# Attention logits as three rounded-float products of high and low parts, with heads 4 to 7 turned late into the slots of heads 0 to 3

## The chip, the cores and the metric

The kernel runs on one core of a Trainium2 chip. The metric is the time of one execution on the device in microseconds (us). Six engines matter: TensorE (PE in the profile; its weight loads are listed apart as PEld), VectorE (DVE), ScalarE (ACT), GpSimd (POOL) and SyncE (SP), which only issues transfers. Each engine works through its own instructions in its own order and waits for others through semaphores.

## The reference

The kernel computes a trunk of two layers on 512 tokens of width 1024: a state-space mixer with a convolutional feed-forward, then shared keys and values, differential attention, and a second feed-forward. The change touches the attention alone. It has 8 heads; each head has two query-key maps of 64 columns (128 columns together) and 128 columns of values. Cut to what matters:

```
k = rms_norm((rms_norm(x) @ kv_w)[:, :1024] as 512 x 8 heads x 2 maps x 64)
v = (rms_norm(x) @ kv_w)[:, 1024:]          as 512 x 8 heads x 128
q = rms_norm((rms_norm(x, ln_g) @ q_w)      as 512 x 8 heads x 2 maps x 64)
logits = einsum('bqhcd,bkhcd->bhcqk', q, k) * 64 ** -0.5 + bias     # causal, c = 2 maps
p = softmax(logits)
attn = p[:, :, 0] - lam * p[:, :, 1]
o = einsum('bhqk,bkhd->bqhd', attn, v)
out = (rms_norm(o) * (1 - lam_init)) @ out_w
```

Queries are worked on in four blocks of 128 tokens. Being causal, block i needs the first (i + 1) x 128 keys: 128, 256, 384 and 512.

## The kernel before, in words

**Precision.** Nearly all large products are not taken in float but in a rounded float type (`fp32r` in the profile, `F32R` in the code). Each operand is split: a high part, the value rounded, made by ScalarE, and a low part, the value less the high part, made by VectorE. Three products (high by high, low by high, high by low) add up in one PSUM bank. The query-key logits are the exception: they are taken in plain float, one matmul for each block and map, which the profile shows as two records.

**PSUM.** There are eight banks of 128 rows x 512 floats: four from `mm_bank`, which hold the running sums of a projection, and four from `aux_bank`, which are handed out in turn to everything else. A bank is handed out again only when the last reader of its earlier content is done.

**Order.** TensorE's order is the order in which the program is written (`manual_schedule`); a scheduler places the instructions of the other engines, mostly in the order of their readiness, and inserts the waits.

**Before the units.** The queries of heads 0 to 3 (`q0`) are projected first. The keys of all heads follow by a seven-product scheme in `keys`: `finish(1, ..)` makes the keys of heads 0 to 3 (`k0`), `finish(0, ..)` those of heads 4 to 7 (`k1`). Values (`v0`, `v1`) and the queries of heads 4 to 7 (`q1`) are projected later, as filling work beside the attention. `head_norm` scales each of the four token blocks of such a set by its reciprocal norms (VectorE), and `turned` then transposes the blocks so that the head's columns lie on the rows of the array: for each token block, TensorE transposes the four heads into one bank (line 1373) and ScalarE evacuates it with a gain (line 1375). `kT[0]`, `qT[0]` hold heads 0 to 3, `kT[1]`, `qT[1]` heads 4 to 7; in both, rows 0-63 belong to map 0 and rows 64-127 to map 1. Where such a pair of blocks is turned is given by `where`: a place inside a projection (`late`). So the turns of `k1` stand within the projection of `v0`, and those of `q1` within that of `v1`. `kT` and `qT` take 32 KB of each of the 128 rows of SBUF.

**The units.** A unit is a head and a part of its query blocks: part 0 is blocks 0 and 1 (128 + 256 keys), part 1 block 2 (384), part 2 block 3 (512). There are 24 units. Each runs through four stages: `logits` (TensorE line 1514, per map one PSUM bank; VectorE adds the bias row `tb` and takes the maximum, line 1520; ScalarE takes the exponential, line 1527), `weigh` (VectorE, line 1537: map 0 less lambda times map 1), `turn` (TensorE transposes the weights into one bank, `at`, line 1546; ScalarE evacuates it, line 1547), and `values` (TensorE multiplies with the values into a bank `po`, line 1557; ScalarE evacuates it into `ot`, line 1560). In a usual step t of the loop, TensorE's order is: `turn` of unit t-2, `logits` of unit t, `values` of unit t-3, then one or more pieces (`next(fill)`) of the filling projections. The first step takes two units at once. A head that is complete is normalized, turned and split (`turned_out`, lines 1583 and 1584), and enters the output projection.

Of the kernel before, what the change touches and what calls it, by code (L numbers as in the profile page):

```python
# [9 lines left out]
F32 = mybir.dt.float32  # L10
# [32 lines left out]
def trunk_kernel(ctx: ExitStack, tc, x, ssm_ln_g, ssm_in_w, ssm_conv_w, ssm_conv_b, ssm_dt_bias,  # L43
# [19 lines left out]
    def aux_bank(name):  # L63
        return pp.tile([P, T], F32, tag="aux", name=name)
# [462 lines left out]
    def run(gen):  # L527
        for _ in gen:
            pass
# [19 lines left out]
    def chain(*gens):  # L549
        for g in gens:  # L550
            yield from g
# [741 lines left out]
    with tc.tile_pool(name="att", bufs=1) as ap, ExitStack() as later:  # L1293
        rts = []
        late = []

        kT = [ap.tile([P, 4, T], F32, name="kT%d" % i) for i in range(2)]
        qT = [ap.tile([P, 4, T], F32, name="qT%d" % i) for i in range(2)]
        vt = [ap.tile([P, D], F32, name="vt%d" % b) for b in range(NT)]

        def key_load(t, j, i, c, **more):
# [51 lines left out]
            act.activation(s, t, AF.Square)  # L1353
            dve.reduce_sum(out[:, b, :], s.rearrange("p (a q) -> p a q", a=8), axis=AX.X)

        def head_norm(key, kn, ss, dst, gcol, where):
            rsqrt_act(ss, ap, key, [P, NT, 8], 64)
            def normed():
                for b in range(NT):
                    v = kn[b].rearrange("p (a q) -> p a q", a=8)  # L1360
                    dve.tensor_tensor(out=v, in0=v, in1=ss[:, b, :].unsqueeze(2).to_broadcast([P, 8, 64]),
                                      op=ALU.mult)

            if key == "q1":
                late.append(((0, 3), normed))
            else:
                normed()

            def turned(bs):
                for b in bs:  # L1370
                    ps = aux_bank("kt%s_%d" % (key, b))
                    for h in range(4):
                        pe.transpose(ps[:, h * P:(h + 1) * P], kn[b][:, h * P:(h + 1) * P], ident)
                    v = ps.rearrange("p (h t) -> p h t", h=4)
                    act.activation(dst[:, :, b * P:(b + 1) * P], v if key[0] == "k" else v[:, :, ::-1],
                                   AF.Copy, scale=c2[:, gcol:gcol + 1])

            for at, bs in zip(where, ((0, 1), (2, 3))):
                late.append((at, lambda bs=bs: turned(bs)))

        def head_sums(key):
            return ap.tile([P, NT, 8], F32, tag="qss", name="ss" + key, bufs=2)

        def qk(key, dst, gcol, where):
# [9 lines left out]
            head_norm(key, kn, ss, dst, gcol, where)  # L1394

        def keys(kc):

# [2 lines left out]

            def first(i, b, ps):
                acc[i][b] = (ap.tile([P, T], F32, tag="kn", name="key%d_%d" % (i, b), bufs=4) if i
                             else qT[1][:, b, :])
                if ps is not None:
                    act.activation(acc[i][b], ps, AF.Copy)

# [69 lines left out]
            finish(0, ((0, 1), (0, 3)))  # L1476

        def vproj(key, i):
            def evac(b, ps, rt):
# [6 lines left out]
        class Unit:  # L1486
# [9 lines left out]
            def logits(self):  # L1496
                h, tag, st = self.h, self.tag, self.st
                if self.part == 0:
                    st["tb"] = up.tile([P, T], F32, tag="tb", name="tb%d" % h, bufs=2)
                    sync.dma_start(st["tb"], bass.AP(tensor=bd.tensor, offset=h * NBIAS + 1, ap=[[1, P], [1, T]]))  # L1500
                    st["sm"] = up.tile([P, NT, 2], F32, tag="sm", name="sm%d" % h, bufs=3)
                i2, h4 = h // 4, h % 4
                k = len(self.ii)
                mx = up.tile([P, k, 2], F32, tag="mx%d" % k, name="mx" + tag, bufs=3)
                self.sm = st["sm"][:, self.ii[0]:self.ii[-1] + 1, :]
                self.p = [up.tile([P, T], F32, tag="p%d" % m, name="lg%s_%d" % (tag, m), bufs=3)
                          for m in range(2)]
                pss = [aux_bank("lg%s_%d" % (tag, m)) for m in range(2)]
                for j, i in enumerate(self.ii):
                    n = (i + 1) * P  # L1510
                    c = slice(self.off[j], self.off[j] + n)
                    for m in range(2):
                        rows = slice(64 * m, 64 * (m + 1))
                        pe.matmul(pss[m][:, c], qT[i2][rows, h4, i * P:(i + 1) * P], kT[i2][rows, h4, :n],
                                  start=True, stop=True)
                for j, i in enumerate(self.ii):
                    n = (i + 1) * P
                    c = slice(self.off[j], self.off[j] + n)
                    for m in range(2):
                        dve.tensor_tensor_reduce(self.p[m][:, c], pss[m][:, c],  # L1520
                                                 st["tb"][:, (3 - i) * P:], 1.0, 3.0e38,
                                                 ALU.add, ALU.min, mx[:, j, m:m + 1])
# [109 lines left out]
            run(rest)  # L1632

        with tc.manual_schedule(engines={mybir.EngineType.PE}):
            run(qk("q0", qT[0], 49, (("2", 1), ("5", 0))))
# [4 lines left out]
            fill = chain(vproj("v0", 0), qk("q1", qT[1], 49, ((2, 0), (2, 1))), vproj("v1", 1),  # L1640
                         attn_out(0, None, range(KB)))
            us = []
            for h in range(AH):
# [125 lines left out]
```

## Time and profile before

| what | value |
|---|---|
| time, median of 3 runs | 1317.85 us (1317.57 to 1318.49) |
| profiled execution, its own time | 1318.13 us |
| span of that execution | 1316.3 us |
| instructions in the profile | 18256 |
| TensorE busy, granted clock | 100% of the span, 1.0 of full speed |
| VectorE, ScalarE, GpSimd busy | 81%, 54%, 14% |
| stage of the units | about 745 to 945 us |
| busy in that stage: TensorE, VectorE, ScalarE | 199.9, 149.7, 139.9 of 200 us |

The page lists busy time by engine, then the span in 40 slices, then the chain of work that ended last, and groups of instructions. A group's row reads: line, engine, operation, output <- inputs (with their tile names), output <- input shapes, x count, busy time, mean nanoseconds of one, idle time of the engine ahead of them. A timeline row reads: start in us, busy time in us, engine, line, operation, names, shapes, x how many in a row; what stands in brackets is the engine's idle time before the row and what ended it. The bias, mask and exponential rows of `lg` carry the same name as the logits' PSUM bank.

### The profile page before, as it was taken

How to read it: one execution, taken by the hardware profiler on the slowest of the kernel's cores; microseconds unless marked ns; L12 is line 12 of the kernel's file. 1: busy time of each engine (PE TensorE's matmuls, PEld its weight loads, DVE VectorE, ACT ScalarE, POOL GpSimd, SP SyncE). 2: the span in 40 equal slices, each digit the busy share in tenths (PEclk: the TensorE clock that was granted, in tenths of full speed). 3: DMA queues.
4: the chain of work that ended last, by engine and by line, in shares of the span. 5: the costliest groups of instructions: out<-in, count | busy, mean ns of one | idle time of the engine just before them, and what ended most of it. 6: DMA issues, size and time to landing. Idle time of an engine off the chain costs nothing.

```text
span 1316.3 us, 18256 instructions
## 1 busy us (share of the span) xinstructions
PE 1311.2 (100%) x6771; PEld 1096.9 (83%) x6771; DVE 1069.5 (81%) x1774; ACT 713.6 (54%) x1156; POOL 178.1 (14%) x244
## 2 busy tenths in 40 slices
PE   9999999999999999999999999999999999999998
PEld 8878888888888988898889887777788888888887
DVE  7989878888878877876888877677778878887886
ACT  6696554743354445544556667767654544544452
POOL 5230200300021401120113210000020100010001
PEclk9999999999999999999999999999999999999999
DMA  7553433432235657673866754211224445453625
GB/s 209 156 153 90 149 101 108 140 95 85 84 96 138 126 139 204 179 161 113 220 164 145 197 124 128 69 60 64 65 80 160 98 119 183 105 96 112 192 64 128
DMA packets 202552, 167.84 MB, mean 128 GB/s; under 512 B 7580, under 2 KB 175904, under 8 KB 202464
## 3 DMA queue, kind: packets, MB, share of 16 engines
q1 hardware_dynamic: 176080, 124.93, 31.7%
q0 software_dynamic: 22928, 36.46, 14.7%
q10 hardware_dynamic: 3456, 5.30, 1.1%
q8 instruction: 53, 0.87, 0.3%
q14 instruction: 35, 0.29, 0.1%
HBM read 160.21 MB, written 6.44 MB: 127 GB/s over the span
## 4 chain that ended last, share of the span: by engine, by line
PE 98%; ACT 1%; DVE 1%; issue 0%; DVEq 0%
PE ps_g L209 6%; PE ps_u L209 6%; PE ps_g L208 6%; PE ps_u L208 6%; PE ps_u L210 6%; PE ps_g L210 6%; PE ps_in L208 5%; PE ps_in L210 5%; PE ps_in L209 5%; PE ps_s L1239 3%; PE ps_s L1244 3%; PE ps_s L1242 3%; PE ps_s L1144 3%; PE ps_s L1146 3%; PE ps_s L1141 3%; PE ps_o L209 2%
## 5 line engine op out<-in xcount | busy, mean ns | idle before, releaser
L208 PE MATMUL ps_u<-xgh,wh_u 128*128 128x512 f32 x352 | 137.4, 390 | 0.0
L209 PE MATMUL ps_g<-xgl,wh_g 128*128 128x512 f32 x352 | 137.1, 390 | 0.0
L208 PE MATMUL ps_g<-xgh,wh_g 128*128 128x512 f32 x352 | 137.1, 389 | 0.0
L210 PE MATMUL ps_u<-xgh,wl_u 128*128 128x512 f32 x352 | 137.0, 389 | 0.0
L209 PE MATMUL ps_u<-xgl,wh_u 128*128 128x512 f32 x352 | 137.0, 389 | 0.0
L210 PE MATMUL ps_g<-xgh,wl_g 128*128 128x512 f32 x352 | 137.0, 389 | 0.0
L208 PE MATMUL ps_in<-xgh,wh_in 128*128 128x512 f32 x304 | 123.0, 404 | 0.0
L210 PE MATMUL ps_in<-xgh,wl_in 128*128 128x512 f32 x304 | 119.7, 394 | 0.0
L209 PE MATMUL ps_in<-xgl,wh_in 128*128 128x512 f32 x304 | 119.2, 392 | 0.0
L209 PEld LDWEIGHTS ps_g<-xgl,wh_g 128*128 128x128 f32 x352 | 66.1, 188 | 13.8 <-DVE xgl L488 0.3
L210 PEld LDWEIGHTS ps_u<-xgh,wl_u 128*128 128x128 f32 x352 | 66.1, 188 | 13.7
L1244 PE MATMUL ps_s<-sl,wh_s 128*128 128x256 f32 x308 | 77.5, 283 | 0.0
L208 PEld LDWEIGHTS ps_g<-xgh,wh_g 128*128 128x128 f32 x352 | 66.1, 188 | 13.7
L1242 PE MATMUL ps_s<-sh,wh_s 128*128 128x256 f32 x308 | 77.5, 283 | 0.0
L210 PEld LDWEIGHTS ps_g<-xgh,wl_g 128*128 128x128 f32 x352 | 66.1, 188 | 13.6
L208 PEld LDWEIGHTS ps_u<-xgh,wh_u 128*128 128x128 f32 x352 | 66.1, 188 | 13.6
L209 PEld LDWEIGHTS ps_u<-xgl,wh_u 128*128 128x128 f32 x352 | 66.1, 188 | 13.5
L1126 ACT ACTIVATE sh<-vg 128x256 fp32r<-128x256 f32 (+1 forms) x44 | 23.1, 524 | 98.5 <-DVE vg L1276 98.4
L1052 POOL DMA_DIRECT2D wz<-in_ffn_down_w_dram x36 | 44.2, 1296 | 235.8 <-DVE wl_s L1080 167.9
L1024 DVE SCALAR_TENSOR_TENSOR vg<-ug,cf,vg 128x511 f32<-128x511 f32 x88 | 65.8, 747 | 5.5 <-ACT vg L1022 4.1
L1272 ACT ACTIVATE vg<-vg 128x512 f32<-128x512 f32 x44 | 27.8, 633 | 78.2 <-DVE vg L1024 78.1
L1021 DVE TENSOR_TENSOR uu<-ps_u,nr_f 128x512 f32<-128x512 f32 x44 | 30.3, 689 | 46.7 <-PE ps_u L210 46.7
(425 smaller groups left out, 3501.2 us busy)
## 6 DMA issues: line engine op xcount, KB each, us to landing
wr_g<-in_ffn_up_w_dram SPq DMA_DIRECT2D x44, 512.0 KB, 3.9
wr_u<-in_ffn_up_w_dram SPq DMA_DIRECT2D x44, 512.0 KB, 3.9
wr_in<-in_ssm_in_w_dram SPq DMA_DIRECT2D x40, 512.0 KB, 3.8
wz<-in_ffn_down_w_dram POOLq DMA_DIRECT2D x27, 512.0 KB, 5.8
m<-cumd POOLq DMA_DIRECT2D x16, 512.0 KB, 4.7
wr_out<-in_ssm_out_w_dram SPq DMA_DIRECT2D x16, 512.0 KB, 3.4
wr_s<-in_ffn_down_w_dram SPq DMA_DIRECT2D x13, 512.0 KB, 3.7
xT<-in_ffn_down_w_dram SPq DMA_DIRECT2D x10, 512.0 KB, 6.8
```

Of the source, the lines that this page charges most:

```text
L208: pe.matmul(ps, wh, xh, start=start, stop=False)
L209: pe.matmul(ps, wh, xl, start=False, stop=False)
L210: return pe.matmul(ps, wl, xh, start=False, stop=stop).ins
L1021: dve.tensor_tensor(out=u, in0=ps, in1=r, op=ALU.mult)
L1024: dve.scalar_tensor_tensor(out=v[:, s:], in0=u[:, :T - s], scalar=col(2 - s), in1=v[:, s:], op0=ALU.mult, op1=ALU.add)
L1052: pool.dma_start(view(t, nq), source(p0, c, nq, j, i), accum_op=ALU.add)
L1141: pe.matmul(pss[b], h, ws[q][1][:, cols], start=False, stop=end and q == qs[-1], skip_group_check=more)
L1144: pe.matmul(pss[b], h, ws[q][0][:, cols], start=first and q == qs[0], stop=False, skip_group_check=more)
L1146: pe.matmul(pss[b], w, ws[q][0][:, cols], start=False, stop=False, skip_group_check=more)
L1239: pe.matmul(v[:, b], wl[:, q, cols], h, start=False, stop=q == nq - 1, skip_group_check=not opens or b > 0)
L1242: pe.matmul(v[:, b], wh[:, q, cols], h, start=opens and q + b == 0, stop=False, skip_group_check=not opens or b > 0)
L1244: pe.matmul(v[:, b], wh[:, q, cols], w, start=False, stop=False, skip_group_check=not opens or b > 0)
```

## The change

**What is computed.** Each float matmul of the logits becomes three rounded matmuls that add up in the same bank: high queries by high keys, low queries by high keys, high queries by low keys. For each of the three, map 0 (rows 0-63) and map 1 (rows 64-127) follow one another. High parts come from ScalarE while it evacuates the turned bank, low parts from VectorE, which reads the same bank.

**Where it is kept.** Four tiles, high and low of keys and queries, now hold four heads only, as large together as `kT` and `qT` were. Heads 0 to 3 fill them first, turned at the same places as before. Turns now go by head: four transposes, one for each token block, into one bank, and one evacuation and one low part behind them. Heads 4 to 7 are turned, one head at a time, into the slot of the head four before them, once that head's last logits are out. The table `turns` sets the step: 4: keys of head 4; 7: keys of head 5; 10: keys of head 6; 11: queries of heads 4 and 5; 13: keys of head 7; 14: queries of head 6; 17: queries of head 7. In a step the turn stands first, ahead of `turn` of unit t-2.

**What moves with it.** The two float arrays for heads 4 to 7 are gone. Until they are turned, the normalized keys of heads 4 to 7 lie in the upper halves of the value tiles (`vt[:, 512:]`), whose values (`v1`) are written last; their sums before normalization lie in the memory of the raw key sums (`whole_sums`) where they lay in `qT[1]`. The queries of heads 4 to 7 lie in their own normalized tiles.

**The diff**, cut to its core:

```
-        kT = [ap.tile([P, 4, T], F32, name="kT%d" % i) for i in range(2)]
-        qT = [ap.tile([P, 4, T], F32, name="qT%d" % i) for i in range(2)]
+        turned_by = {n: [ap.tile([P, 4, T], F32R, name=n + "T_" + x) for x in ("hi", "lo")] for n in "kq"}
+        second = {}
...
-        def head_norm(key, kn, ss, dst, gcol, where):
+        def turn_head(kind, h, src):
+
+            ps = aux_bank("kt%s%d" % (kind, h))
+            for b in range(NT):
+                pe.transpose(ps[:, b * P:(b + 1) * P], src[b][:, h % 4 * P:(h % 4 + 1) * P], ident)
+            g = c2[:, 48:49] if kind == "k" else c2[:, 49:50]
+            v, hi, lo = (t.rearrange("p (b t) -> p b t", b=NT) for t in [ps] + [t[:, h % 4] for t in turned_by[kind]])
+            if kind == "q":
+                v = v[:, :, ::-1]
+            act.activation(hi, v, AF.Copy, scale=g)
+            dve.scalar_tensor_tensor(out=lo, in0=v, scalar=g, in1=hi.bitcast(F32), op0=ALU.mult, op1=ALU.subtract)
+
+        def head_norm(key, kn, ss, where, to=None):
...
-            def turned(bs):
-                for b in bs:
-                    ps = aux_bank("kt%s_%d" % (key, b))
-                    for h in range(4):
-                        pe.transpose(ps[:, h * P:(h + 1) * P], kn[b][:, h * P:(h + 1) * P], ident)
-                    v = ps.rearrange("p (h t) -> p h t", h=4)
-                    act.activation(dst[:, :, b * P:(b + 1) * P], v if key[0] == "k" else v[:, :, ::-1],
-                                   AF.Copy, scale=c2[:, gcol:gcol + 1])
-
-            for at, bs in zip(where, ((0, 1), (2, 3))):
-                late.append((at, lambda bs=bs: turned(bs)))
+            if key[1] == "1":
+                second[key[0]] = to
+                return
+            for at, hs in zip(where, ((0, 1), (2, 3))):
+                late.append((at, lambda hs=hs: [turn_head(key[0], h, to) for h in hs]))
...
-                head_norm(key, acc[i], ss, kT[1 - i], 48, where)
+                head_norm(key, acc[i], ss, where, None if i else [v[:, T:] for v in vt])
...
-                    for m in range(2):
-                        rows = slice(64 * m, 64 * (m + 1))
-                        pe.matmul(pss[m][:, c], qT[i2][rows, h4, i * P:(i + 1) * P], kT[i2][rows, h4, :n],
-                                  start=True, stop=True)
+                    for z, (q, k) in enumerate(((qh, kh), (ql, kh), (qh, kl))):
+                        for m in range(2):
+                            rows = slice(64 * m, 64 * (m + 1))
+                            pe.matmul(pss[m][:, c], q[rows, h4, i * P:(i + 1) * P], k[rows, h4, :n],
+                                      start=z == 0, stop=z == 2)
...
+            turns = {4: "k4", 7: "k5", 10: "k6", 11: "q4 q5", 13: "k7", 14: "q6", 17: "q7"}
...
+                for x in turns.get(t, "").split():
+                    turn_head(x[0], int(x[1]), second[x[0]])
                 turn_to(t - 1)
```

**TensorE's order** in step 4 (unit 4 is head 1, part 1). `at0_2` is the turned weights of head 0, part 2; `lg1_1_0` and `lg1_1_1` are the logits of head 1, part 1, map 0 and 1; `po0_1` is the product with the values of head 0, part 1. Before:

```order
L1546 MATMUL at0_2_7824<-ident_77,lg0_2_0_7734 128x128 x4
L1514 MATMUL lg1_1_0_7833<-kT0_6903,qT0_6905 128x384
L1514 MATMUL lg1_1_1_7834<-kT0_6903,qT0_6905 128x384
L1557 MATMUL po0_1_7845<-vt0_6907,at0_1_7768 128x128
L1557 MATMUL po0_1_7845<-vt1_6908,at0_1_7768 128x128
L1557 MATMUL po0_1_7845<-vt2_6909,at0_1_7768 128x128
```

With the change, where `ktk4` is the bank into which the keys of head 4 are turned:

```order
L1360 MATMUL ktk4_7831<-ident_77,vt3_6910 128x128
L1555 MATMUL at0_2_7839<-ident_77,lg0_2_0_7742 128x128 x4
L1523 MATMUL lg1_1_0_7848<-kT_hi_6903,qT_hi_6905 128x384
L1523 MATMUL lg1_1_1_7849<-kT_hi_6903,qT_hi_6905 128x384
L1523 MATMUL lg1_1_0_7848<-kT_hi_6903,qT_lo_6906 128x384
L1523 MATMUL lg1_1_1_7849<-kT_hi_6903,qT_lo_6906 128x384
L1523 MATMUL lg1_1_0_7848<-kT_lo_6904,qT_hi_6905 128x384
L1523 MATMUL lg1_1_1_7849<-kT_lo_6904,qT_hi_6905 128x384
L1566 MATMUL po0_1_7864<-vt0_6907,at0_1_7768 128x128
```

The four transposes of the turn (the last of them is the first row) stand ahead of `at0_2`, and the two float matmuls have become six rounded ones; the values product behind them is as it was.

**ScalarE's order** in the same step: `ot0` is the output of head 0, evacuated from `po0_0` and `po0_1`; rows of `lg` and `sm` are the exponentials. Before:

```order
L1560 ACTIVATE ot0_7797<-po0_0_7798 128x256
L1547 ACTIVATE at0_2_7823<-at0_2_7824 128x512
L1527 ACTIVATE lg1_1_0_7831,sm1_7776<-lg1_1_0_7831,mx1_1_7830 128x384
L1527 ACTIVATE lg1_1_1_7832,sm1_7776<-lg1_1_1_7832,mx1_1_7830 128x384
L1560 ACTIVATE ot0_7797<-po0_1_7845 128x128
```

With the change:

```order
L1569 ACTIVATE ot0_7805<-po0_0_7806 128x256
L1365 ACTIVATE kT_hi_6903<-ktk4_7831,c2_89 128x512
L1556 ACTIVATE at0_2_7838<-at0_2_7839 128x512
L1536 ACTIVATE lg1_1_0_7846,sm1_7776<-lg1_1_0_7846,mx1_1_7845 128x384
L1536 ACTIVATE lg1_1_1_7847,sm1_7776<-lg1_1_1_7847,mx1_1_7845 128x384
L1569 ACTIVATE ot0_7805<-po0_1_7864 128x128
```

The high part of the turned keys has come in directly ahead of the evacuation of `at0_2`.

**The order of transfers on SP's queue** around the first units: `tb0`, `tb1` are the bias rows of heads 0 and 1, `wr_q1_0` to `wr_q1_6` the raw weights for the queries of heads 4 to 7. Before:

```order
L140 DMA wr_q1_0_7560<-in_q_w_dram 128x2x512
L1500 DMA tb0_7638<-bd_3652 128x512
L1500 DMA tb1_7774<-bd_3652 128x512
L140 DMA wr_q1_2_7616<-in_q_w_dram 128x2x512
L140 DMA wr_q1_4_7695<-in_q_w_dram 128x2x512
L140 DMA wr_q1_6_7803<-in_q_w_dram 128x2x512
```

With the change:

```order
L140 DMA wr_q1_0_7564<-in_q_w_dram 128x2x512
L140 DMA wr_q1_2_7624<-in_q_w_dram 128x2x512
L140 DMA wr_q1_4_7715<-in_q_w_dram 128x2x512
L140 DMA wr_q1_6_7811<-in_q_w_dram 128x2x512
L1507 DMA tb0_7646<-bd_3652 128x512
L1507 DMA tb1_7774<-bd_3652 128x512
```

The two bias rows have moved behind three weight loads; in the changed program `tb0` lies where the sums of the keys of heads 4 to 7 lay, and so its transfer waits for the last instruction that reads them, VectorE's write of the normalized keys of token block 3.

More of the change, by code (lines that the diff above doesn't have):

```diff
@@ L1354, in squared @@
             dve.reduce_sum(out[:, b, :], s.rearrange("p (a q) -> p a q", a=8), axis=AX.X)
-        def head_norm(key, kn, ss, dst, gcol, where):
+        def turn_head(kind, h, src):
[9 more added lines that the diff above has]
+        def head_norm(key, kn, ss, where, to=None):
             rsqrt_act(ss, ap, key, [P, NT, 8], 64)
+            to = to or kn
             def normed():
                 for b in range(NT):
-                    v = kn[b].rearrange("p (a q) -> p a q", a=8)
-                    dve.tensor_tensor(out=v, in0=v, in1=ss[:, b, :].unsqueeze(2).to_broadcast([P, 8, 64]),
+                    v, o = (t[b].rearrange("p (a q) -> p a q", a=8) for t in (kn, to))
+                    dve.tensor_tensor(out=o, in0=v, in1=ss[:, b, :].unsqueeze(2).to_broadcast([P, 8, 64]),
                                       op=ALU.mult)
@@ L1367, in head_norm, with qk @@
                 normed()
-            def turned(bs):
-                for b in bs:
-                    ps = aux_bank("kt%s_%d" % (key, b))
-                    for h in range(4):
-                        pe.transpose(ps[:, h * P:(h + 1) * P], kn[b][:, h * P:(h + 1) * P], ident)
-                    v = ps.rearrange("p (h t) -> p h t", h=4)
-                    act.activation(dst[:, :, b * P:(b + 1) * P], v if key[0] == "k" else v[:, :, ::-1],
-                                   AF.Copy, scale=c2[:, gcol:gcol + 1])
-            for at, bs in zip(where, ((0, 1), (2, 3))):
-                late.append((at, lambda bs=bs: turned(bs)))
+            if key[1] == "1":
[3 more added lines that the diff above has]
+                late.append((at, lambda hs=hs: [turn_head(key[0], h, to) for h in hs]))
         def head_sums(key):
             return ap.tile([P, NT, 8], F32, tag="qss", name="ss" + key, bufs=2)
-        def qk(key, dst, gcol, where):
+        def qk(key, where=()):
             kn, ss = [], head_sums(key)
@@ L1393, in qk @@
             yield from proj(key, evac)
-            head_norm(key, kn, ss, dst, gcol, where)
+            head_norm(key, kn, ss, where)
         def keys(kc):
@@ L1475, in keys @@
                     finish(1, ((4, 0), (4, 2)))
-            finish(0, ((0, 1), (0, 3)))
+            finish(0, ())
         def vproj(key, i):
@@ L1501, in logits @@
                     st["sm"] = up.tile([P, NT, 2], F32, tag="sm", name="sm%d" % h, bufs=3)
-                i2, h4 = h // 4, h % 4
+                (kh, kl), (qh, ql) = (turned_by[n] for n in "kq")
+                h4 = h % 4
                 k = len(self.ii)
@@ L1634, in trunk_kernel @@
         with tc.manual_schedule(engines={mybir.EngineType.PE}):
-            run(qk("q0", qT[0], 49, (("2", 1), ("5", 0))))
+            run(qk("q0", (("2", 1), ("5", 0))))
             with tc.tile_pool(name="keys", bufs=1) as kc:
@@ L1639, in trunk_kernel @@
             up = later.enter_context(tc.tile_pool(name="units", bufs=1))
-            fill = chain(vproj("v0", 0), qk("q1", qT[1], 49, ((2, 0), (2, 1))), vproj("v1", 1),
+            fill = chain(vproj("v0", 0), qk("q1"), vproj("v1", 1),
                          attn_out(0, None, range(KB)))
```

2 lines of the change are left out of this document (1 added, 1 removed).

## The prediction

> **What bounds the kernel now.** I read the page first, then the groups of instructions kept apart by shape, then the timeline of the attention stage, where the change lies.
>
> ```profile
> span 1316.3 us, 18256 instructions
> PE 1311.2 (100%) x6771; PEld 1096.9 (83%) x6771; DVE 1069.5 (81%) x1774; ACT 713.6 (54%) x1156; POOL 178.1 (14%) x244
> PEclk9999999999999999999999999999999999999999
> PE 98%; ACT 1%; DVE 1%; issue 0%; DVEq 0%
> ```
>
> TensorE is busy all the span, at the full clock, and is 98% of the chain that ended last. So a matmul that gets shorter moves the end by as much, and every time TensorE is made to wait moves it back. The groups of the logits (line 1514), and below them a float and a rounded-float matmul of equal size:
>
> ```profile
> L1514 PE MATMUL lg<-kT,qT 64*128 64x512 f32 x32 | 9.2, 641 | 0.0
> L1514 PE MATMUL lg<-kT,qT 64*128 64x384 f32 x32 | 7.2, 528 | 0.0
> L1514 PE MATMUL lg<-kT,qT 64*128 64x256 f32 x32 | 5.1, 378 | 0.0
> L1514 PE MATMUL lg<-kT,qT 64*128 64x128 f32 x32 | 4.2, 322 | 0.0
> L784 PE MATMUL st<-xe,bt 128*128 128x512 f32 x10 | 5.1, 592 | 0.0
> L208 PE MATMUL ps_g<-xgh,wh_g 128*128 128x512 f32 x352 | 137.1, 389 | 0.0
> ```
>
> One float matmul stands in the trace as two records (32 of each size for 16 products). 32 records of 641 ns would be 20.5 us end to end and cover only 9.2: the two softmax maps, which use rows 0-63 and 64-127 of the array, run at the same time. A float record of 512 columns is 0.20 us longer than a rounded one. The timeline of the three kinds of unit (two short query blocks; 384 keys; 512 keys):
>
> ```profile
> 829.92 0.60 PE L1546 MATMUL at<-ident,lg 128*128 128x128 f32 x4
> 830.45 0.92 PE L1514 MATMUL lg<-kT,qT 64*128 64x384 f32 x4
> 830.62 0.60 ACT L1547 ACTIVATE at<-at 128x512 f32<-128x512 f32 x1 [1.56 <-PE at L1546]
> 831.30 0.94 PE L1557 MATMUL po<-vt,at 128*128 128x128 f32 x6
> ...
> 834.84 0.49 PE L1546 MATMUL at<-ident,lg 128*128 128x128 f32 x3
> 835.25 1.13 PE L1514 MATMUL lg<-kT,qT 64*128 64x512 f32 x4
> 835.25 0.30 PEld L1514 LDWEIGHTS lg<-kT,qT 64*128 64x128 f32 x4 [0.17 <-issue]
> ...
> 836.31 1.16 PE L1557 MATMUL po<-vt,at 128*128 128x128 f32 x8
> ...
> 840.49 0.93 PE L1514 MATMUL lg<-kT,qT 64*128 64x128 f32 x8
> 841.34 0.94 PE L1557 MATMUL po<-vt,at 128*128 128x128 f32 x6
> ```
>
> From start to start the logits hold TensorE 0.85, 1.06 and 0.85 us, 2.76 a head, 22.1 us for eight. TensorE is not kept waiting in this stage.
>
> **The logits, rounded.** Two pairs of records become three pairs. Going from 384 to 512 columns costs 1.06 - 0.85 = 0.21 us for two pairs, so 0.82 ns a column and pair; then 0.85 - 2 x 384 x 0.82 ns leaves 0.22 us of entering and leaving, which stays. For the rounded pair I take the steady spacing of full-width rounded matmuls, from the chain in order of time (four of 512 columns, four of 256), and for 128 columns that of the transposes:
>
> ```profile
> 752.67 0.91 PE ps_K L1446 x4
> 561.86 0.48 PE ps_s L1239 x4
> 818.67 1.04 PE L1373 MATMUL ktk<-ident,qT 128*128 128x128 f32 x8
> 819.30 1.26 ACT L1375 ACTIVATE kT<-ktk,c 128x512 f32<-128x512 f32 x2 [1.03 <-PE ktk L1373]
> 819.54 0.49 PE L1546 MATMUL at<-ident,lg 128*128 128x128 f32 x3
> 820.46 0.49 ACT L1547 ACTIVATE at<-at 128x384 f32<-128x384 f32 x1
> ```
>
> That is 0.227 us for 512, 0.12 for 256, hence 0.173 for 384; eight transposes take 819.54 - 818.67, 0.11 each. The new slots: 0.22 + 3 x (0.11 + 0.12) = 0.91; 0.22 + 3 x 0.173 = 0.74; 0.22 + 3 x 0.227 = 0.90. A head takes 2.55 instead of 2.76: -1.7 us in all, the short blocks even losing 0.06. If the fixed part is 0.20, it is -2.2. I take **-1.9**. No row shows rounded matmuls of 64 rows, so the other end is that the two maps don't overlap: six matmuls one after the other, 1.60 + 1.26 + 1.58 = 4.44 a head, +13.4 us. I take the overlap, since the float pairs have it, and the pairs again alternate between the two halves of the array.
>
> **Low parts.** Sixteen subtractions on VectorE come in, one a head for keys and queries; like line 1584 they read PSUM with a per-partition gain:
>
> ```profile
> L1583 ACT ACTIVATE oh<-oT,c x8: 667/682/689, 848.5 to 945.4; 128x512 fp32r<-128x512 f32 x8
> L1584 DVE SCALAR_TENSOR_TENSOR ol<-oT,c,oh x8: 741/748/752, 849.4 to 946.1; 128x512 fp32r<-128x512 f32 x8
> sum 200.00, PE 199.92 PEld 157.04 DVE 149.65 ACT 139.89 POOL 7.21; mean PE 10.00 PEld 7.85 DVE 7.48 ACT 6.99 POOL 0.36
> ```
>
> 16 x 0.75 = 12 us on an engine that is busy 150 of 200 us from 745 to 945 (last row): hidden where nobody waits for it. ScalarE's sixteen evacuations stay sixteen of 0.68 us.
>
> **The moved turns.** 64 transposes stay 64. The two blocks of eight for keys of heads 4 to 7 and the two for queries go (0.87 us each with what follows); eight groups of four come back at 0.43, all beside an existing group `at`: -0.1 us. But each new group stands directly ahead of `at` in a unit, and its evacuation stands ahead of that of `at` on ScalarE. Four banks serve `at`, two logits and `po`; with the turn a step needs five, and in the built program `po` then waits for the evacuation of the `at` of its own step (before: mostly for an older bank). PE's steps at 384 keys, as they are from 1.38 us: 0.43 turn, 0.53 `at`, 0.74 logits, so `po` could start at 1.70. ScalarE: an evacuation starts 819.30 - 818.67 = 0.63 after the first transpose, the next 0.58 later (two in 820.46 - 819.30), and `at` takes 0.60: 1.81. So `po` is 0.11 late for k4 and k7. Where ScalarE is already late for `at`, all is later:
>
> ```profile
> 844.86 0.60 PE L1546 MATMUL at<-ident,lg 128*128 128x128 f32 x4
> 845.69 0.58 ACT L1547 ACTIVATE at<-at 128x512 f32<-128x512 f32 x1
> 860.25 0.60 PE L1546 MATMUL at<-ident,lg 128*128 128x128 f32 x4
> 861.27 0.58 ACT L1547 ACTIVATE at<-at 128x512 f32<-128x512 f32 x1
> 885.59 0.49 PE L1546 MATMUL at<-ident,lg 128*128 128x128 f32 x3
> 885.79 1.06 ACT L148 ACTIVATE wh_ao<-wr_ao 128x1024 fp32r<-128x1024 f32 x1 [1.02 <-PE ps_v L1337]
> 886.75 0.47 ACT L1547 ACTIVATE at<-at 128x384 f32<-128x384 f32 x1
> ```
>
> At k5's place ScalarE is free 0.83 after the step's start, 0.31 late with the change; at k6's 1.02, 0.50 late; at q6's 1.16 (a weight half ahead of it): 1.16 + 0.58 + 0.47 = 2.21 against 0.43 + 0.41 + 0.90 = 1.74, 0.47 late; q7 not late. At unit 11 q4 and q5 stand together, and the second map's logits take q4's bank: they wait for its low part, 0.63 + 0.68 + 0.75 = 2.06 against 0.86 + 0.41 = 1.27, 0.79 late. Sum 0.11 + 0.31 + 0.50 + 0.11 + 0.79 + 0.47 = 2.3 us, with a hand-over of some 0.08 at each 2.9; I take **+2.6**. Below, the wait is nothing if ScalarE takes a turn in its idle 1.56 us before `at`; above, see the rivals. Behind a late `po` stand the projection's matmuls, so the delay passes whole to the end.
>
> **A table moved on SP's queue.** The bias rows of heads 0 and 1 are now issued behind three weight loads, and wait for the last write of normalized keys, which are read from the memory they land in.
>
> ```profile
> 805.70 2.50 DVE L1361 TENSOR_TENSOR qT<-qT,ssk 128x512 f32<-128x512 f32 x4
> 812.51 0.29 DVE L1520 CUSTOM_DVE_ANT_0 lg<-lg,tb 128x128 f32<-128x128 f32 x1 [1.40 <-PE lg L1514]
> 815.20 0.75 DVE L1537 SCALAR_TENSOR_TENSOR lg<-lg,sm,lg 128x128 f32<-128x128 f32 x2
> tb<-bd SPq DMA_DIRECT2D x4, 256.0 KB, 4.5
> ```
>
> The writes end at 808.2, with a low part between at 808.9; 4.5 us to landing is 813.4, so the first logits' bias add starts 0.9 us late, and the weighing ends near 816.9 instead of 815.95. The transposes that read it stand at 819.54, less 0.87 for the removed block: 818.67. Hidden, with 1.7 us to spare; a landing above 6.2 us would uncover it. The first key sums move to the memory of the raw key sums, whose readers, the low parts of those sums, stand ahead of them in the program; nothing.
>
> **Sum.** -1.9 - 0.1 + 2.6 = +0.6 us on the profiled execution's 1318.13 us, whose span is 1316.3. That execution is 0.28 us above the median, 1317.85; I carry the difference over: **1318.5 us**.
>
> [...]
>
> **Rivals.** (a) *Three quarters everywhere*: if entering and leaving shrink too and 128 columns follow the columns rather than 0.11 us, logits go to 16.6 us: 1317.85 - 5.5 - 0.1 + 2.6 = 1314.9, and less where the waits are short. For it: a float record is two rounded ones long. Against: loads of 128 columns at 0.11, four of them alone in 0.30 us in the PEld row. (b) *The waits vanish*, since ScalarE slips the turn in early: 1315.9, within 0.2% of before. Against: it is in `at`'s way by order. (c) *Slower by the turned banks*: at each of the seven places the evacuation finds ScalarE on a weight half of some 0.7 us or on a row of exponentials, as two of the places already do; with 0.4 us more each, 2.6 + 2.8 gives 1321.3. It decides from 0.66 us a place. For it: the lateness of 0.31 to 0.50 read above; against: 1.56 us idle at k4's. (d) *No overlap of the maps*: +13.4, the waits for `po` then mostly covered, 0.8 left at unit 11: 1331.9.
>
> **How the numbers follow.** Forecast 0.57 (own range 1317 to 1320), (b) 0.10, (a) with its neighbours 0.12, (c) 0.14, (d) 0.07. What one can tell from no change is about 0.2%, 2.6 us. Faster is (a): 0.12; within is the forecast and (b): 0.67; slower is (c) and (d): 0.21. The range 1315.3 to 1321.3 leaves out (d), most of (a), and the upper part of (c).
>
> **What would show it.** The slots from first logits to `po` should be 0.9, 0.74 and 0.9 us where no turn stands. Records of the two maps should start in twos; if they start one by one, (d). At k5, k6, q6 TensorE should have gaps of 0.3 to 0.5 us ahead of `po`, and ahead of the second map's logits at unit 11 near 0.8, released by ScalarE's `at` and VectorE's low part. VectorE should gain 12 us, ScalarE nothing. The forecast is wrong if those gaps sum to over 4.6 or if the logits' slots fall below 2.4 us a head.

## The result

| | median | runs | lowest to highest |
|---|---|---|---|
| before | 1317.93 us | 13 | 1317.52 to 1319.52 |
| with the change | 1320.91 us | 13 | 1319.34 to 1321.93 |

The ratio is 1.0021, with a 95% interval of 1.0012 to 1.0029: the change costs 1.6 to 3.8 us. The forecast was 1318.5 us, in a range of 1315.3 to 1321.3; the time lies in the range, 2.4 us above the forecast.

The profiled execution of the change takes 1320.91 us, its span is 1319.2 us, 2.9 more than before. From its page:

```profile
span 1319.2 us, 18395 instructions
PE 1310.2 (99%) x6835; PEld 1100.3 (83%) x6835; DVE 1085.9 (82%) x1790; ACT 713.7 (54%) x1156; POOL 177.7 (13%) x244
PE 94%; ACT 2%; DVE 2%; DMA 1%; issue 1%; DVEq 0%; SPq 0%; POOLq 0%; ACTq 0%
```

TensorE is busy 1 us less, but the chain that ended last now runs through it for 94% and not 98%: the shares of ScalarE and VectorE have grown from 1% to 2% each, and 1% of DMA has come in. The view of TensorE's waits says where (what it waited for; us in total, times, longest; the two smallest rows, of 0.2 us each, are left out). Before, the row of `warm`, from the program's start, stood there alone:

```profile
PE po L1566 <- ACT at L1556: 1.7, 3, 0.8
PE warm L292 <- DVE ones L219: 1.1, 1, 1.1
PE lg L1523 <- DVE mx L1529: 0.7, 1, 0.7
PE ps_s L1144 <- ACT wh_s L1079: 0.4, 1, 0.4
PE lg L1523 <- DVE qT_lo L1366: 0.4, 1, 0.4
PE po L1566 <- DVE ol L1593: 0.3, 1, 0.3
```

**The logits.** The timeline of TensorE at three units where it waits for nothing: 512 keys, 384 keys, and two short blocks:

```profile
833.54 0.49 PE L1523 MATMUL lg<-kT_hi,qT_hi 64*128 64x512 f32 x2
...
834.43 1.16 PE L1566 MATMUL po<-vt,at 128*128 128x128 f32 x8
...
897.22 0.44 PE L1523 MATMUL lg<-kT_hi,qT_hi 64*128 64x384 f32 x2
...
897.94 0.94 PE L1566 MATMUL po<-vt,at 128*128 128x128 f32 x6
...
906.48 0.33 PE L1523 MATMUL lg<-kT_hi,qT_hi 64*128 64x128 f32 x2
...
907.37 0.82 PE L1566 MATMUL po<-vt,at 128*128 128x128 f32 x5
```

The slots, from the first logits to `po`, are 0.89, 0.72 and 0.89 us: 2.50 a head where it was 2.76, 2.1 us less for eight. The two maps of a product stand in one row (x2) and run together: the 16 records of the first product of 512 columns, 0.49 us each, cover 4.6 us and not 7.9.

**The turns.** One of them, the keys of head 6:

```profile
859.02 0.60 PE L1360 MATMUL ktk<-ident,vt 128*128 128x128 f32 x4
...
859.98 0.44 PE L1523 MATMUL lg<-kT_hi,qT_hi 64*128 64x384 f32 x2
...
860.40 0.67 ACT L1365 ACTIVATE kT_hi<-ktk,c 128x512 fp32r<-128x512 f32 x1
...
860.97 0.59 ACT L1556 ACTIVATE at<-at 128x512 f32<-128x512 f32 x1
...
861.61 0.49 PE L1566 MATMUL po<-vt,at 128*128 128x128 f32 x2 [0.84 <-ACT at L1556]
```

ScalarE comes to the turned keys 1.38 us after the step's start, then to `at`, and TensorE stands 0.84 us before `po` until `at` is out of its bank. The slot is 1.63 in place of 0.72. All seven places, from the same timeline:

| turn | slot from, to (us) | slot | more than undisturbed | forecast |
|---|---|---|---|---|
| k4 | 828.67, 829.57 | 0.90 | 0.18 | 0.11 |
| k5 | 843.99, 845.15 | 1.16 | 0.44 | 0.31 |
| k6 | 859.98, 861.61 | 1.63 | 0.91 | 0.50 |
| q4 and q5 | 869.63, 871.39 | 1.76 | 0.87 | 0.79 |
| k7 | 880.94, 881.84 | 0.90 | 0.18 | 0.11 |
| q6 | 886.66, 888.07 | 1.41 | 0.52 | 0.47 |
| q7 | 902.78, 903.68 | 0.90 | 0.01 | 0 |

They sum to 3.1 us.

**The last units.** A third part the forecast did not have. In the timeline of the change, TensorE around unit 0 and unit 1 of head 7, and behind it VectorE in the same stretch:

```profile
920.43 0.33 PE L1523 MATMUL lg<-kT_hi,qT_hi 64*128 64x128 f32 x2
...
921.70 0.94 PE L1566 MATMUL po<-vt,at 128*128 128x128 f32 x6 [0.31 <-DVE ol L1593]
923.87 0.60 PE L1555 MATMUL at<-ident,lg 128*128 128x128 f32 x4
925.15 0.92 PE L1523 MATMUL lg<-kT_hi,qT_hi 64*128 64x384 f32 x2 [0.69 <-DVE mx L1529]
...
926.35 0.82 PE L1566 MATMUL po<-vt,at 128*128 128x128 f32 x5
...
922.89 1.22 DVE L159 TENSOR_TENSOR wl_ao<-wr_ao,wh_ao 128x1024 fp32r<-128x1024 f32 x1
924.03 0.16 DVE L501 TENSOR_TENSOR rst_o<-so 128x4 f32<-128x4 f32 x1
924.10 0.28 DVE L1529 CUSTOM_DVE_ANT_0 lg<-lg,tb 128x128 f32<-128x128 f32 x1
...
925.62 0.42 DVE L1529 CUSTOM_DVE_ANT_0 lg<-lg,tb 128x256 f32<-128x256 f32 x1
```

Before, the same instructions of VectorE stood in another order:

```profile
921.20 0.28 DVE L1520 CUSTOM_DVE_ANT_0 lg<-lg,tb 128x128 f32<-128x128 f32 x1
...
921.79 0.16 DVE L501 TENSOR_TENSOR rst_o<-so 128x4 f32<-128x4 f32 x1
...
922.16 0.41 DVE L1520 CUSTOM_DVE_ANT_0 lg<-lg,tb 128x256 f32<-128x256 f32 x1
...
922.58 1.22 DVE L159 TENSOR_TENSOR wl_ao<-wr_ao,wh_ao 128x1024 fp32r<-128x1024 f32 x1
```

With the change the low half of a weight (`wl_ao`, 1.22 us) and a step of head 5's normalization (`rst_o`, which needs two answers of ScalarE) come ahead of the bias adds of head 7, and these free the banks that the next logits need. Against undisturbed steps, TensorE is late 0.38 (slot of 1.27 from 920.43), 0.75 (from `at` to logits 1.28, usually 0.53) and 0.48 (slot of 1.20): 1.6 us, with 0.18 a step earlier 1.8. Before, one slot here was 0.15 late, so the change adds 1.6. The last units can be measured as a whole: from the `po` at 912.15 to the last `po` at 931.64 TensorE takes 19.5 us. Before, it took 18.3 (911.02 to 929.31), though the logits in it were longer.

The account of the profiled pair: -2.1 logits, +3.1 turns, +1.6 last units, +0.4 a wait of the second feed-forward for a weight half (`ps_s <- ACT wh_s` above), +0.1 already there when the units begin: +3.1, against 2.9 in the spans.

### The profile page after: what moved, and what is told of

It reads as the page before. It is cut to its first block, busy times and chain, and to the rows that moved or that the text cites. A ratio compares the mean times of both kernels' runs of the same rounds, so it can differ in the third digit from the quotient of the medians.

```text
span 1319.2 us, 18395 instructions
## 1 busy us (share of the span) xinstructions
PE 1310.2 (99%) x6835; PEld 1100.3 (83%) x6835; DVE 1085.9 (82%) x1790; ACT 713.7 (54%) x1156; POOL 177.7 (13%) x244
## 4 chain that ended last, share of the span: by engine, by line
PE 94%; ACT 2%; DVE 2%; DMA 1%; issue 1%; DVEq 0%; SPq 0%; POOLq 0%; ACTq 0%
PE ps_g L209 6%; PE ps_u L210 6%; PE ps_g L210 6%; PE ps_u L209 6%; PE ps_u L208 6%; PE ps_g L208 6%; PE ps_in L208 5%; PE ps_in L210 5%; PE ps_in L209 5%; PE ps_s L1239 3%; PE ps_s L1244 3%; PE ps_s L1242 3%; PE ps_o L209 2%; PE ps_o L210 2%; PE ps_o L208 2%; PE ps_s L1144 2%
```

## The experiments

The theory after these readings: two losses, each with its own cause, eat the gain of the logits. The first is ScalarE's order behind each late turn. The second is VectorE's order in the last units, which comes out otherwise when the logits are rounded: of the two programs of the first two experiments, the one with float logits has `wl_ao` behind the bias adds as before, the one with rounded logits ahead of them. The main rival puts the second loss on the turns and low parts.

**The late turns alone.**

```
-    turned_by = {n: [ap.tile([P, 4, T], F32R, name=n + "T_" + x) for x in ("hi", "lo")] for n in "kq"}
+    turned_by = {n: [ap.tile([P, 4, T], F32R if x == "lo" else F32, name=n + "T_" + x)
+                     for x in ("hi", "lo")] for n in "kq"}
...
-    for z, (q, k) in enumerate(((qh, kh), (ql, kh), (qh, kl))):
-        for m in range(2):
-            rows = slice(64 * m, 64 * (m + 1))
-            pe.matmul(pss[m][:, c], q[rows, h4, i * P:(i + 1) * P], k[rows, h4, :n],
-                      start=z == 0, stop=z == 2)
+    for m in range(2):
+        rows = slice(64 * m, 64 * (m + 1))
+        pe.matmul(pss[m][:, c], qh[rows, h4, i * P:(i + 1) * P], kh[rows, h4, :n],
+                  start=True, stop=True)
```

> The late turns and the low parts alone: the logits are taken in plain float from the high tiles, which here hold the turned keys and queries unrounded; the low parts are still made but no product reads them. Theory: the slots of the logits are those of before (0.85, 0.85, 1.06 us), so the waits behind the turns shrink by what these slots are longer: k4 and k7 0.05 each, k5 0.3, k6 0.8, q4 with q5 0.7, q6 0.35, in all 2.2 us; the last units from 914 us on run as before, because with float logits VectorE's order there is that of before: 1320.1 us. Rival (the 1.6 us lost in the last units come from the sixteen low parts or the turns, which load VectorE and ScalarE): the same waits and the last units late as well, 1321.7 us.

Measured: 1319.89 us, ratio to before 1.0014 (1.0005 to 1.0023). The only waits of TensorE in the stage are those behind turns:

```profile
PE po L1566 <- ACT at L1556: 0.9, 3, 0.5
```

The slots at the turns are longer than undisturbed float slots by 0.05, 0.22, 0.54, 0.86, 0.05 and 0.35 us, 2.1 in all. The last units run as before, in 18.3 us. So the turns and the low parts don't delay them: the rival falls.

**The rounded logits alone.**

```
-    kT = [ap.tile([P, 4, T], F32, name="kT%d" % i) for i in range(2)]
-    qT = [ap.tile([P, 4, T], F32, name="qT%d" % i) for i in range(2)]
+    kT = [ap.tile([P, 4, T], F32R, name="kT%d" % i) for i in range(2)]
+    qT = [ap.tile([P, 4, T], F32R, name="qT%d" % i) for i in range(2)]
...
+    for z in range(3):
         for m in range(2):
             rows = slice(64 * m, 64 * (m + 1))
             pe.matmul(pss[m][:, c], qT[i2][rows, h4, i * P:(i + 1) * P], kT[i2][rows, h4, :n],
-                      start=True, stop=True)
+                      start=z == 0, stop=z == 2)
```

This edits the kernel before; the sums and the normalized keys of heads 4 to 7 lie in the memory that the change gave them.

> The rounded logits alone: both sets of heads are turned early as before into eight rounded slots, there are no low parts, and the three products all take the high parts (so the logits come out as three times the product of the high parts: the low parts are left out). Theory: logits -2.1 us, no waits behind turns, but VectorE's order in the last units is that of the change (the low half of a weight ahead of the bias adds of the last head), so 1.6 us are lost there again: 1317.9 - 2.1 + 1.6 = 1317.4 us. Rival (the last units are late because of the turns and low parts): nothing lost there, 1315.8 us.

Measured: 1318.47 us, ratio 1.0002 (0.9993 to 1.0011). Its waits in the stage are those of the last units, with no late turn and no low parts of keys or queries in the program:

```profile
PE lg L1516 <- DVE mx L1522: 0.7, 1, 0.7
PE po L1559 <- DVE ol L1586: 0.3, 1, 0.3
```

Step by step against before, its TensorE gains 1.8 us from the first logits to the `po` that stood at 914.66 before, and gives back 1.2 of them by 929. So the gain of the rounded logits is real, and most of it is lost again in the last units, which take 19.3 us. The median says that more is lost than the 1.2, and the expected 1317.4 us was too low; but the profiled execution (1317.55 us) is the fastest of eleven, and at 1 us the interval can't tell.

**The turn behind the weights' transposes.**

```
-                for x in turns.get(t, "").split():
-                    turn_head(x[0], int(x[1]), second[x[0]])
                 turn_to(t - 1)
+                for x in turns.get(t, "").split():
+                    turn_head(x[0], int(x[1]), second[x[0]])
```

> The change, with each late turn one place further: behind the transposes of the weights (at) instead of ahead of them, so ScalarE evacuates at first. Still five banks are needed in such a step. Theory (the wait is ScalarE's order, the high part in the way of at): the waits at k4, k5, k6, k7 and q6 go, and 0.7 us stay where q4 and q5 stand together, since po then takes q4's bank and waits for its low part: 3.1 us of waits become 0.7, 1318.5 us. Rival (a fifth bank is wanted in any place of the step, and ScalarE is late in these steps whatever comes first): about 1320.5 us or more.

Measured: 1318.37 us, ratio 1.0003 (0.9994 to 1.0012). The same step still needs five banks, the same instructions are issued, and 2.5 us of the 3.1 are gone: what was paid for was the place on ScalarE's queue, which follows the place on TensorE's. What is left of the late slots is 0.33 at k6, where none was expected, and 0.31 at q4 with q5, where 0.7 was. A wait of 0.3 that the change did not have has come in (`oT <- DVE kT_lo`).

**The turn behind the values.**

```
                 values_to(t - 2)
+                for x in turns.get(t, "").split():
+                    turn_head(x[0], int(x[1]), second[x[0]])
                 for i in range(places):
```

(and the two lines gone ahead of `turn_to`.)

> The change, with each late turn behind the values product (po) of its step, ahead of the filling projection, whose 3 us hide the evacuation and the low part. Theory: no wait behind a turn is left, 3.1 us less than the change: 1317.8 us, of which the last units still cost 1.6. Rival (the turns cost by themselves, as extra groups on TensorE and extra work on ScalarE and VectorE, wherever they stand): between 1319.5 and 1321 us.

Measured: 1317.84 us, ratio 0.9997 (0.9988 to 1.0006), 3.1 below the change. The place of k6, where the slot was 1.63:

```profile
859.35 0.44 PE L1523 MATMUL lg<-kT_hi,qT_hi 64*128 64x384 f32 x2
...
860.07 0.94 PE L1566 MATMUL po<-vt,at 128*128 128x128 f32 x6
...
860.29 0.58 ACT L1556 ACTIVATE at<-at 128x512 f32<-128x512 f32 x1
```

The slot is 0.72 though `at` is evacuated only after `po` has begun: with four banks in use ahead of it, `po` no longer needs the bank of its own step's `at`. A turn so placed costs TensorE hardly more than its transposes. The expectation's 3 us of projection behind it are not the same everywhere: behind k6's transposes 6.0 us of other work follow before the next step (861.33 to 867.35), behind q7's only 1.5 (902.15 to 903.62), and the next slots are undisturbed there too (0.91 and 0.89).

**VectorE's order in the last units, one half of it.**

```
                 self.high()
-                self.low()
+                with tc.issue_after(state["biased"]) if self.key == "ao1_0" else nullcontext():
+                    self.low()
```

(`biased` is the latest bias add of a unit.)

> The change, with one thing put back on VectorE: the low half of the weight ao1_0 (1.22 us) stands behind the bias adds of the first unit of head 7 again, as before, instead of ahead of them; no other engine's order differs. Theory (the last units are late because VectorE's order was turned there): the wait of 0.7 us for a bank that the bias adds free goes, and the weights and values products that follow come 1 to 1.3 us earlier: 1320.9 - 1.2 = 1319.7 us. Rival (the last units are bound by the chain through the exponentials, in whatever order the low half stands): 1320.9 us.

> Both cures: each late turn behind the values product of its step, and the low half of ao1_0 behind the bias adds. Theory (the waits behind the turns and VectorE's order in the last units are separate losses and add up): 1317.84 of the turns' cure alone less 1.1 to 1.2, 1316.7 us, faster than before by some 1.3 us, most of the 2.1 us that the logits gain. Rival (once the one wait is gone the other takes its place): 1317.5 to 1318 us.

> The rounded logits alone, early turns, three products of the high parts (low parts left out), and the low half of ao1_0 behind the bias adds. Theory: with VectorE's order mended the logits' gain of 2.1 us reaches the end: 1318.1 - 2.1 = 1316.0 us. Rival (the gain is lost to other work further on, whatever the order): within 0.5 us of 1318.1.

Measured: on the change itself 1320.27 us, ratio 1.0019 (1.001 to 1.0028); with the turns behind the values 1317.46, 0.9996 (0.9988 to 1.0005); with the rounded logits alone 1316.83, 0.9993 (0.9984 to 1.0002). In the profiles the wait of 0.7 us for `mx` is gone, and in all three another stands in its place:

```profile
PE lg L1517 <- ACT ot L1563: 0.9, 1, 0.9
```

(of the last of the three). All three came out 0.6 to 0.8 us above the time that their theory gave, and of the second the rival held: once the one wait is gone, the other takes its place. Moving the low half alone cured little. By the medians it is worth 0.6, 0.4 and 1.6 us against the program without this edit, each uncertain by over 1; in the traces the last units take 19.3, 19.0 and 19.1 us, 0.2 less in each. VectorE, with both cures, still stood idle in front of head 5's normalization, with the bias adds behind it:

```profile
918.61 0.15 DVE L499 SCALAR_TENSOR_TENSOR rsm_o<-so,eps 128x4 f32<-128x4 f32 x1
919.27 0.16 DVE L502 TENSOR_TENSOR rst_o<-so 128x4 f32<-128x4 f32 x1 [0.51 <-ACT so L501]
...
919.59 0.29 DVE L1530 CUSTOM_DVE_ANT_0 lg<-lg,tb 128x128 f32<-128x128 f32 x1
```

**VectorE's order, both halves.** The last part of head 5's normalization is written behind the logits of unit 0 of head 7:

```
+            def scaled():
                 rsqrt_act(so, ap, "o%d" % h, [P, NT], P, e)
                 dve.tensor_tensor(out=ot, in0=ot, in1=so.unsqueeze(2).to_broadcast([P, NT, P]), op=ALU.mult)
+            if h == 5:
+                state["scaled"] = scaled
+            else:
+                scaled()
...
                     us[t].logits()
+                if t == n - 3:
+                    with tc.issue_after(state["biased"]):
+                        state.pop("scaled")()
```

> Late turns behind the values product, the low half of ao1_0 behind the bias adds of unit 0 of head 7, and now also the last part of head 5's normalization (which waits for two trips to ScalarE, and ahead of which VectorE stood 0.5 us idle in the run with both cures) behind them. Theory (what still delays the last units is the normalization standing ahead of the bias adds: the first of these starts 0.9 us later than it could, the last 1.2): the wait of 0.9 us for the bank behind ScalarE's evacuation goes, 1317.5 - 0.9 = 1316.6 us. Rival (these units are bound by their own chain of bias, exponential, weighing and evacuation): 1317.5 us.

> The change itself, turns where it has them, with VectorE's order in the last units mended in the same two places (the low half of ao1_0 and head 5's normalization behind the bias adds). Theory: 3.1 us of waits behind the turns stay, the last units lose 0.3 instead of 1.3 us: 1320.9 - 1.1 = 1319.8 us, and TensorE's trace shows no wait for a bank at the first logits of unit 1 of head 7. Rival (bound by their own chain): 1320.5 us, with such a wait in another place.

Measured: with the turns behind the values 1316.03 us, ratio 0.9988 (0.998 to 0.9997), faster than before; on the change itself 1319.56, ratio 1.0012 (1.0003 to 1.0021). The first of the two, VectorE and then TensorE:

```profile
920.05 0.28 DVE L1530 CUSTOM_DVE_ANT_0 lg<-lg,tb 128x128 f32<-128x128 f32 x1
...
920.82 0.42 DVE L1530 CUSTOM_DVE_ANT_0 lg<-lg,tb 128x256 f32<-128x256 f32 x1
...
921.23 1.22 DVE L159 TENSOR_TENSOR wl_ao<-wr_ao,wh_ao 128x1024 fp32r<-128x1024 f32 x1
...
921.09 0.60 PE L1556 MATMUL at<-ident,lg 128*128 128x128 f32 x4
921.62 0.44 PE L1524 MATMUL lg<-kT_hi,qT_hi 64*128 64x384 f32 x2
...
922.65 0.94 PE L1567 MATMUL po<-vt,at 128*128 128x128 f32 x6 [0.25 <-ACT ot L1570]
```

The logits follow `at` without a wait (0.53). Not all is cured: 0.3 us of the slot of 1.03 remain as a loss, and 0.25 in the step before (917.79 to 918.93, with a wait of 0.2 for `ol`).

By the medians the turns' place is worth 3.1 us, VectorE's order 1.4 (on the change) or 1.8 (with the turns moved), and with both the kernel is 1.9 us faster than before, in an interval of 0.4 to 2.6. The traces say less of VectorE's order. The last units take 18.4 us with the turns moved (19.2 without this edit) and 18.7 on the change itself (19.5): 0.8 us come back in both. So about half of the 1.6 us is shown to be the order of these two pieces; the rest still stands in the two slots above, and no run shows what holds it. From the first logits to the last `po`, the run with all cures takes 116.2 us where before took 117.8: 1.5 of the logits' 2.1 us reach the end of the stage.

**The maps apart.** The last question was whether the two maps run together because they follow one another in the order.

```
-    for z, (q, k) in enumerate(((qh, kh), (ql, kh), (qh, kl))):
-        for m in range(2):
+    for m in range(2):
+        for z, (q, k) in enumerate(((qh, kh), (ql, kh), (qh, kl))):
```

> The change, with the products of map 0 all ahead of those of map 1, so that neighbours in the order mostly use the same rows of the array. Theory (two maps run at once only where they follow one another directly): at 512 columns five slots of 0.227 instead of three, +0.45 us, at 384 +0.35, at 128 and 256 together some +0.35; 1.15 a head and 9.2 in all, of which the waits behind the turns hide about 2.5: 1327.6 us. Rival (the array finds the overlap by itself, in whatever order): 1320.9 us.

Measured: 1319.93 us, ratio 1.0013 (1.0004 to 1.0022), no slower than the change. The theory's 1327.6 fell; the rival's 1320.9 was close. A unit of two short blocks in its timeline:

```profile
822.58 0.33 PE L1523 MATMUL lg<-kT_hi,qT_hi 64*128 64x128 f32 x2
822.75 0.28 PE L1523 MATMUL lg<-kT_hi,qT_lo 64*128 64x128 f32 x2
...
823.48 0.38 PE L1566 MATMUL po<-vt,at 128*128 128x128 f32 x1
```

The maps still start in twos, though in the program map 1's first product is now the fourth. In the next run, with all cures, all of map 0 stands ahead of all of map 1, six products in a unit of two blocks:

> All cures, and in each unit all products of map 0 (three, or six in a unit of two query blocks) ahead of all of map 1. Theory, from the run with the maps apart, where three products ahead changed nothing (the two halves of the rows take their matmuls from the order independently): the records of the two maps still start in twos, the slots stay 0.9, 0.72 and 0.89 us, and the time is that of the run with all cures, 1316.0 us, but for small changes of VectorE's order. Rival (only a few instructions ahead are looked at, fewer than six): the units of two blocks run partly one map after the other, 0.89 grows to some 1.2 us, 1318.5 us.

Measured: 1319.36 us, ratio 1.0009 (0.9999 to 1.0019), 3.3 above the run with all cures. The same kind of unit:

```profile
824.05 0.32 PE L1524 MATMUL lg<-kT_hi,qT_hi 64*128 64x128 f32 x1
824.21 0.27 PE L1524 MATMUL lg<-kT_hi,qT_lo 64*128 64x128 f32 x1
824.32 0.27 PE L1524 MATMUL lg<-kT_lo,qT_hi 64*128 64x128 f32 x1
824.33 0.44 PE L1524 MATMUL lg<-kT_hi,qT_hi 64*128 64x128 f32 x2
...
825.21 0.38 PE L1567 MATMUL po<-vt,at 128*128 128x128 f32 x1
```

Map 1's first product, seventh in the order, starts with map 0's third (its row of two takes in map 0's first product of 256 keys), and the slot is 1.16 in place of 0.89: 2.2 us for eight heads. So the rival held. Of the other 1.1 us, 0.8 stand in the last unit's slot (1.69 in place of 0.89), where `po` waits 0.7 for `ol` and not 0.2. Why is not shown; VectorE's order differs from the run with all cures.

## Why the prediction was right or wrong

- **The logits**: -1.9 forecast, -2.1 measured. The slots of 0.91, 0.74 and 0.90 came out as 0.89, 0.72 and 0.89; the fixed 0.22 us was 0.02 too long. The rival of three quarters everywhere fell: the slots are 0.84 (512), 0.85 (384) and 1.05 (two short blocks) of those before. The Trainium skill (FP8 and Floating Point Precision, TensorE Precision Notes) has four passes for a true float product; if a rounded product took one such pass, which that section does not say, three would take 0.75 of the time. This trace agrees at no width. The rival without overlap fell too.
- **The waits behind the turns**: +2.6 forecast, +3.1 measured, the mechanism as described, and shown by moving the turn by one place on ScalarE. The one place that was clearly mis-sized is k6: 0.50 forecast, 0.91 measured. The forecast took ScalarE to come free as long after the step's start as before, 1.02 us. It was 1.38: TensorE began this step 1.23 us earlier than before (859.02 against 860.25), ScalarE came free only 0.87 earlier (860.40 against 861.27).
- **The table on SP's queue**: hidden, as forecast; the step's 0.9 us of lateness wasn't there, since the rows land in 3.3 us where 4.5 was taken.
- **The low parts**: 16 of 0.744 us, 11.9 in all, as forecast, with no delay of the last units (the run of the late turns alone). Four transposes take 0.43 us (859.02 to 859.45), as forecast.
- **What failed**: the sum had no term for the last units. It read the stage from 902 us on as the rest of it ("TensorE is not kept waiting in this stage"), and asked what each added instruction would delay, not whether the scheduler would put the old instructions of VectorE in another order. It did, and the last units lost 1.6 us, the larger part of the 2.4 between forecast and measurement. Some 0.8 of them came back in the traces when two pieces of that order were mended; what holds the rest stays open. Rival (c) named nearly the measured time, 1321.3, but for a cause that wasn't there: the turns' waits are 3.1, not 5.4.
- **Luck**: the time lies outside the forecast's own range of 1317 to 1320. It lies inside the wider one only because that was drawn up to rival (c)'s time, for a loss of another kind.
- **The chances**: 0.67 stood on no change beyond 0.2%; measured is 0.21% (0.12 to 0.29), on the border to the case that had 0.21.
- **Left open**: the 0.4 us in the second feed-forward. It is in the profiles of most runs with late turns and not in those of the three programs without, and no experiment here tells why. Open, too, is what holds the last units once VectorE's order is mended. Nor is it shown why the scheduler turns VectorE's order when the logits are rounded; shown is that the programs with rounded logits have the new order and those with float ones the old.

## What to carry to other kernels

A piece of work that is added to a full engine's step costs what stands behind it on the evacuating engine: put it where nothing behind it is due soon (here behind the values product, by the medians 3.1 us cheaper for the same instructions). When a scheduler orders the other engines, compare their whole order before and after, in stages that the change doesn't touch too, above all where the slack is small. A gain on the bounding engine reaches the end only if the steps after it were not already at the pace of another engine.

## What the runs showed that was not expected

The two halves of TensorE's rows take their matmuls from the order with some independence. With three products of rows 0-63 ahead of three of rows 64-127, the two halves still start together and the slot is unchanged, 0.89 us; with six ahead the second half starts with the third product of the first, 0.28 us late, and the slot is 1.16. The Trainium skill (TensorE: Matmul & The Clock Gate, Part 3: Packing small matmuls) has weight loads pulled ahead of matmuls in flight when they use other rows, and matmuls themselves starting strictly in order. The first fits: in the run with three ahead, the weights of the first and the fourth product load together at 822.58, those of the second at 822.69. The second doesn't fit the starts measured here, where the fourth product in the order starts together with the first, at 822.58, and ahead of the second, at 822.75. (The records don't name the map. But a block has only two products of high parts by high parts, one for each map, so the two in one row are one of each.)

The independence ends at a wait. At q4 and q5 in the change, map 1's first product waits for its bank:

```profile
869.63 0.50 PE L1523 MATMUL lg<-kT_hi,qT_hi 64*128 64x512 f32 x1
870.50 0.49 PE L1523 MATMUL lg<-kT_hi,qT_hi 64*128 64x512 f32 x1 [0.37 <-DVE qT_lo L1366]
870.51 0.72 PE L1523 MATMUL lg<-kT_hi,qT_lo 64*128 64x512 f32 x2
```

Map 0's second product, whose operands and bank were there by 869.63, starts only at 870.51, with map 1's.
